# Second layer of a two-layer encoder: two projection chunks of 1024 columns in place of four of 512, rotation in place, attentions that take items as quarters come

## The chip, the cores and the metric

The kernel runs on one core of one Trainium2 chip. The metric is the device time of one execution in microseconds (us). A core has a matrix engine (TensorE, PE in the profile; its weight loads are PEld), VectorE (DVE), ScalarE (ACT), GpSimd (POOL) and a queue that only starts transfers (SP). Each works through its own instructions in order and waits for others by semaphores.

## The reference

Two layers over 512 tokens of width 1024, with 256 memory tokens. The second layer, which the change is about:

```python
h = rmsnorm(x, norm_g[i]); mem_h = rmsnorm(mem, mem_norm_g[i])
proj = einsum('bsd,de->bse', h, w_in_b)      # q 8 heads | k 2 | v 2 | q_mem 4 | gate 12, heads of 128
# mixer_axial_gqa, four q heads to one k/v head
q = rmsnorm(q, qn_g); k = rmsnorm(k, kn_g)
q = apply_rope(q, ang) * 128**-0.5; k = apply_rope(k, ang)
o_mix = softmax(q @ k.T) @ v
# memory_attention, 4 heads
q = rmsnorm(q_mem, qn) * 128**-0.5; k = rmsnorm(kv_k, kn)
o_mem = softmax(q @ k.T) @ kv_v
y = concatenate([o_mix, o_mem]) * silu(gate)
x = x + y @ w_out[i]
```

## The kernel before

All float32 products are made of three float32r matmuls (`mm3`: high x high, high x low, low x high), so every operand is split into a high part (a cast on ScalarE) and a low part (a subtraction on VectorE). For weights these are `wh` and `wo`, tiles of 128 x 1024.

The large projections run as *chunks* (`s_chunk`). A chunk takes the 512 tokens in two halves i and its columns in two halves j, so it has four quarters of output, named "11", "12", "21", "22" by i and j. It makes them with seven products (Winograd's form of Strassen's multiplication), in the order 12, 11, S1, S2, S4, S3, 22, on two accumulators in PSUM (`pj`). After a product `keep` copies the accumulator on ScalarE, or `add` combines it with a kept copy on VectorE (`sn<-pj,sn`); a quarter that is finished goes into its evaluation `ev`. Products S2, S4 and S3 go on accumulating in a bank that an eviction has read. Quarter 11 is finished after the second product, 12 after the fifth, 22 after the sixth, 21 after the seventh.

A product is cut into *slots*. A chunk of 512 columns (n = 256) has one slot per product: 24 matmuls that move 256 columns. A chunk of 1024 columns (n = 512) has two slots per product: 12 matmuls of 512 columns each. Each slot uses one pair `wh`, `wo`. Class `Weights` streams them: `dma` loads 512 KB tiles (`wl`) on SP's queue while fewer than `KEEP` of the chunk's kind live; the products T1 to T4 need sums of quarters, which `sum` makes with adding transfers on GpSimd's queue (T1 and T3 add from DRAM, `wl<-in_wall_dram`; T2 and T4 add from another tile, `wl<-wl`); `hi` and `lo` split them. `PLAN` lists the chunks' kinds.

Class `Driver` interleaves all else. After a slot's matmuls `tick` steps every spawned generator once, and up to two of the `later` ones; a `yield n` sleeps n slots. `drv.late` puts work at the end of the tick, `drv.soon` at the start of the next. So what stands in each engine's queue is set by this order alone. In the gate chunks a and b every third slot has a half tick more (`HALF`), which steps the first of the `later` generators.

The second layer has 79 slots: 8 for the memory's keys and values (`mem_kv`), four chunks of 512 columns for q_mem, k with v, and q in two halves, three gate chunks of 512 columns (m for the four memory heads, a for heads 0 to 3, b for heads 4 to 7), 14 slots of seven products of the output projection (`out_proj`) for the memory heads and heads 0 to 3, and 8 for the rest of it (`out_rest`, heads 4 to 7). Attentions are pipelines (`pipeline`) of five steps, one item per step:

- `score` on TensorE (`sb`; `sm` for memory); `top` takes the row maximum on VectorE (`nmb`, `nmm`);
- `exps` on ScalarE (`pb`, `pm`); `scale` on VectorE (`rdb` and `pb`; `rdm` and `pm`);
- `turn` transposes on TensorE (`ptb`, `pmt`), split by ScalarE and VectorE into `pbT`, `pmT`;
- `pv` on TensorE (`ob`, `om`), `out_` copies to `o` on ScalarE, and a transfer stores it in DRAM (`odb<-o`).

The attention of the mixer (`attn_b`) has 32 items, four blocks of 128 tokens in each of eight heads, in the order of the heads. The memory attention has eight. The evaluation of a gate quarter loads the stored outputs again (`og<-odb`) once they are there, and multiplies them in (`yf`). `prep_y` makes the seven operands of the output projection from `yf`: y12 and y11 need only the first half of the tokens, the others (`ys`, then `yS`) both halves. `rope_b` rotates q and k with the tables `ropeB` (tile `tabs`), which `setup_b` makes on GpSimd at the beginning of the layer.

Of the kernel before, what the change touches and what calls it, by code (L numbers as in the profile page):

```python
# [30 lines left out]
YB = {"m": (2, 2), "k": (1, 1, 1), 0: (1, 2, 1), 1: (1, 2, 1)}  # L31
# [4 lines left out]
PLAN = ["W2"] + ["T2"] * 2 + ["W1", "W2s"] + ["W2" if c.isdigit() else "W1" for c in A_ORDER[1:]] + ["W2"] + ["O1"] * 2 + ["T2b"] * 2 + ["W1b"] * 7 + ["W2b"] + ["O1"] * 2  # L36
T1_DMA = 17
KEEP = {"T2": 6, "T2b": 4, "O1": 4, "W1": 9, "W2": 10, "W2s": 9, "W1b": 7, "W2b": 9}
# [71 lines left out]
def trunk_kernel(ctx: ExitStack, tc: tile.TileContext, x, mem, wall, norm_g, mem_norm_g, gcol,  # L110
# [48 lines left out]
    LOADS = (("21", "21"), ("11", "11"), ("T1", "12"), ("T2", "22"), ("22", "22"), ("T3", "12"))  # L159
    GROUPS = {"T2": (2, 2), "T2b": (2, 2), "O1": (1, 4)}  # L160

    class Weights:
        def __init__(self):
# [3 lines left out]
            for c, kind in enumerate(PLAN):  # L167
                base = len(self.items)
                if kind in GROUPS:
                    units, nb = GROUPS[kind]  # L170
                    for u in range(units):
                        for x in (2 * u, 2 * u + 1):
                            self.items.append((c, "P", x))
                            self.last.append(g + (u + 1) * nb - 1)
                            self.allocs.append(((c, "P", x), d, kind))
                            self.users[c, "P", x] = 1
                            d += 1
                        self.need += [base + 2 * u + 2] * nb
                    g += units * nb
                else:  # L180
                    n = 1 if kind in ("W1", "W1b") else 2
                    at = {k: d + i * n for i, k in enumerate(("21", "11", "12", "22"))}
                    d += 4 * n
                    self.allocs += [((c, k, x), at[q] + x, kind) for k, q in LOADS for x in range(n)]
                    for k in ORDER:
                        for x in range(n):
# [3 lines left out]
                            if k[0] == "T":  # L190
                                self.sums.append(((c, k, x), at["11" if k == "T1" else "22"] + x))
# [17 lines left out]
        def dma(self, most=9):  # L209
            while self.allocs and self.live < KEEP[self.allocs[0][2]] and most:  # L210
# [7 lines left out]
                nc.sync.dma_start(self.tile[key], wall[d])  # L218
# [4 lines left out]
        def sum(self, force=False, want=None):  # L223

            for n, (key, d) in enumerate(self.sums[:8]):
# [3 lines left out]
                if k == "T1" and c >= T1_DMA:  # L229
                    if not self.ripe(self.load_at, key, force):  # L230
                        continue
                    G.dma_start(self.tile[key], wall[d], accum_op=ALU.add)
# [10 lines left out]
                elif k == "T3":  # L243
                    if not self.ripe(self.load_at, key, force):
                        continue
                    G.dma_start(self.tile[key], wall[d], accum_op=ALU.add)
# [84 lines left out]
    def s_chunk(n, act, ev, tokens=True, pre=None, half=False):  # L331
# [5 lines left out]
        def keep(name, u, b):  # L337
# [3 lines left out]
            if name == "s3":  # L341
                c = snap["s5", u]
                V.tensor_tensor(c, c, t, ALU.subtract)
                yield 1
                yield from ev("22", u, c)

        def add(q, name, u, b):
            t = snap[name, u]
            V.tensor_tensor(t, b, t, ALU.subtract if q == "12" else ALU.add)  # L349
            yield 1  # L350
# [3 lines left out]
        for i, (a, s, fresh) in enumerate(PRODUCTS):  # L354
# [4 lines left out]
            for x in range(units):  # L359
                wh, wo = [t.rearrange("p (k c) -> p k c", c=n) for t in W.take()]  # L360
                ah, al = act[a][:, 0], act[a][:, 1]
                for b in range(2):
# [6 lines left out]
                    o = bank[s][b] if units == 2 else bank[s][0][:, b * 256:(b + 1) * 256]  # L369
                    bs = slice(b * 128, (b + 1) * 128)  # L370
# [215 lines left out]
    def pipeline(n, *stages, ready=None, step=1):  # L586

        last = max(k for k, _, _ in stages)
        for t in range(n + last):
            while ready and t < n and not ready(t):  # L590
                yield 1
            for k, f, late in stages:
                if 0 <= t - k < n:
                    if late:
                        drv.late(lambda f=f, i=t - k: f(i))
                    else:
                        f(t - k)
            yield step

    def mem_attn(qm, km, vm, put, step):  # L600

        sc, pr, pts, tp, oo = {}, {}, {}, {}, {}

        def score(i):
            h, b2 = divmod(i, 2)
            sp = sc[i] = at("sm").rearrange("p (b k) -> p b k", b=2)
            for j in range(2):
                cs = slice((2 * b2 + j) * 128, (2 * b2 + j + 1) * 128)
                mm3(sp[:, j, :], qm[h // 2][0][:, h % 2, cs], qm[h // 2][1][:, h % 2, cs], km[0][:, h, :], km[1][:, h, :], True, True)
# [33 lines left out]
        def pv(i):  # L643
            h, b2 = divmod(i, 2)
            p = pts.pop(i)
            if b2 == 0:
# [6 lines left out]
        def out_(i):  # L653
            h, b2 = divmod(i, 2)
            if b2:
                os = put(h)
                A.copy(os, oo.pop(h))
                put(h, os)

        yield from pipeline(8, (0, score, 0), (4, pv, 0), (3, turn, 0), (2, scale, 0), (1, exps, 0),  # L660
                            (0, top, 1), (3, hi, 1), (3, lo, 1), (4, out_, 1), step=step)
# [20 lines left out]
    def gates(od, o_done):  # L682
# [3 lines left out]
        def gate(H, first, g, half=False):  # L686
# [6 lines left out]
            def ev(q, u, t):  # L693
# [7 lines left out]
                o = load() if {h0, h0 + 1} <= o_done else None  # L701
# [5 lines left out]
                if not o:  # L707
                    while not {h0, h0 + 1} <= o_done:
# [184 lines left out]
    def put_od(i, t=None):  # L893
# [3 lines left out]
        o_done.add(i)  # L897
# [20 lines left out]
    def mem_a():  # L918
        while seen[0] < 4:
            yield 1  # L920
        yield from mem_attn(qm, km, vm, lambda h, t=None: put_od(8 + h, t), MEM_STEP[0])
# [270 lines left out]
    def put_ob(i, t=None):  # L1192
# [279 lines left out]
```

## Time and profile before

| | |
|---|---|
| median of 3 timed runs | 997.8 us (997.62 to 1000.34) |
| the profiled execution: its time | 1000.03 us |
| the profiled execution: its span | 998.3 us |
| mean granted TensorE clock | 0.993 |
| TensorE, VectorE, ScalarE, GpSimd busy | 955.1, 821.6, 644.5, 340.2 us |
| first 256-wide matmul of the second layer | at 690.82 us |

A line of a timeline gives the start, the duration, the engine, the source line, the operation, the tiles written and read with their shapes, and in brackets the idle time before it with what ended it. A line of the groups gives the count after x, the busy time with the mean of one in ns, and the idle time before. A matmul's duration is a latency: the next one starts before it ends.

### The profile page before, as it was taken

To read this page: it belongs to the slowest core of one execution; us is meant where nothing else is said; L and a number is where in the kernel's file an instruction comes from. 1 tells how busy PE (TensorE), PEld (TensorE's weight loads), DVE (VectorE), ACT (ScalarE), POOL (GpSimd) and SP (SyncE) were. 2 spreads that over 40 slices of the span, in tenths; PEclk is the share of its full clock that TensorE was granted. 3 is DMA by queue.
4 is the path that set the end of the run, shared out by engine and by line. 5 is a ranking of instruction groups with operands and counts; after the bars stand their busy time and mean duration, and the time that the engine had idled before them with its cause. 6 is when DMAs were issued, how large, how long until landed. Compare 5 with 4: busy or idle time off the path is not lost.

```text
span 998.3 us, 16623 instructions
## 1 busy us (share of the span) xinstructions
PE 955.1 (96%) x5724; PEld 839.7 (84%) x5724; DVE 821.6 (82%) x1487; ACT 644.5 (65%) x1623; POOL 340.2 (34%) x470
## 2 busy tenths in 40 slices
PE   7899999999999999999999979999999999998998
PEld 4778988887888888888899967888999989987886
DVE  5787678778878787878888898978879898889974
ACT  4566568676768685858685646556667666667650
POOL 1232424665545454545544020223632331011000
PEclk9999999999999999999999999999999999999999
DMA  9969946959595949585949695759784876777432
GB/s 336 296 199 352 279 99 159 308 111 277 122 281 120 282 118 283 124 277 126 273 103 312 181 273 150 274 214 336 194 190 117 228 174 166 207 200 170 134 127 85
DMA packets 86966, 206.13 MB, mean 206 GB/s; under 512 B 25057, under 2 KB 35809, under 8 KB 86882
## 3 DMA queue, kind: packets, MB, share of 16 engines
q1 hardware_dynamic: 70034, 146.28, 41.3%
q0 software_dynamic: 15552, 56.63, 30.1%
q10 hardware_dynamic: 1296, 2.16, 0.6%
q8 instruction: 45, 0.74, 0.3%
q14 instruction: 39, 0.32, 0.1%
HBM read 157.79 MB, written 12.65 MB: 171 GB/s over the span
## 4 chain that ended last, share of the span: by engine, by line
PE 55%; DVE 14%; DMA 3%; ACT 3%; issue 3%; POOL 1%; SPq 0%; DVEq 0%; ACTq 0%; POOLq 0%
PE pj L149 13%; PE pj L148 13%; PE pj L150 13%; DVE wo L277 4%; PE oo L1102 1%; PE pt L1081 1%; DVE wl L236 1%; PE qT L512 1%; PE sa L1000 1%; DMA oth<-ds 1%; PE ptb L1304 1%; DVE sn L349 1%; DMA wl<-wl 1%; POOL tabs L1182 1%; PE xT L442 1%
## 5 line engine op out<-in xcount | busy, mean ns | idle before, releaser
L277 DVE TENSOR_TENSOR wo<-wl,wh 128x1024 fp32r<-128x1024 f32 x255 | 316.3, 1244 | 10.2 <-ACT wh L267 9.9
L267 ACT CAST wh<-wl 128x1024 fp32r<-128x1024 f32 x255 | 267.6, 1056 | 41.2 <-PE pj L150 20.8
L148 PE MATMUL pj<-wh,hS 128*128 128x512 f32 (+1 forms) x448 | 164.9, 368 | 4.3 <-DVE sn L349 3.3
L149 PE MATMUL pj<-wo,hS 128*128 128x512 f32 (+1 forms) x448 | 158.8, 354 | 2.7 <-DVE wo L277 2.6
L150 PE MATMUL pj<-wh,hS 128*128 128x512 f32 (+1 forms) x448 | 158.7, 354 | 0.0
L149 PE MATMUL pj<-wo,h 128*128 128x512 f32 (+1 forms) x336 | 120.1, 358 | 6.5 <-DVE wo L277 6.5
L148 PE MATMUL pj<-wh,h 128*128 128x512 f32 (+1 forms) x336 | 123.6, 368 | 1.7 <-ACT h L142 1.7
L150 PE MATMUL pj<-wh,h 128*128 128x512 f32 (+1 forms) x336 | 119.6, 356 | 0.0
L391 POOL TENSOR_TENSOR rstd<-mse,half 128x4 f32<-128x4 f32 (+2 forms) x98 | 106.3, 1085 | 8.2
L148 PEld LDWEIGHTS pj<-wh,hS 128*128 128x128 f32 x448 | 85.2, 190 | 14.9 <-DVE sn L349 3.8
L149 PEld LDWEIGHTS pj<-wo,hS 128*128 128x128 f32 x448 | 85.5, 191 | 13.9 <-DVE wo L277 4.1
L150 PEld LDWEIGHTS pj<-wh,hS 128*128 128x128 f32 x448 | 85.3, 190 | 12.1
L500 ACT ACTIVATE junk<-sn 128x128 f32<-128x128 f32 x264 | 78.9, 304 | 20.8 <-DVE sn L349 19.7
L390 POOL TENSOR_SCALAR mse<-hss 128x4 f32<-128x4 f32 (+1 forms) x86 | 47.9, 557 | 109.8 <-ACT junk L500 105.3
L149 PEld LDWEIGHTS pj<-wo,h 128*128 128x128 f32 x336 | 64.3, 191 | 16.5 <-DVE wo L277 9.1
L339 ACT COPY sn<-pj 128x512 f32<-128x512 f32 x132 | 72.5, 584 | 8.2 <-PE pj L150 8.2
L251 POOL DMA_DIRECT2D wl<-wl x33 | 29.8, 903 | 131.1 <-DVE wo L277 70.3
L944 POOL TENSOR_TENSOR ta<-sn,tabs 128x128 f32<-128x128 f32 (+1 forms) x64 | 36.5, 571 | 109.6 <-DVE sn L505 76.9
L148 PEld LDWEIGHTS pj<-wh,h 128*128 128x128 f32 x336 | 64.3, 192 | 9.5 <-ACT h L142 2.1
L150 PEld LDWEIGHTS pj<-wh,h 128*128 128x128 f32 x336 | 64.2, 191 | 9.0 <-DVE h L145 0.2
L349 DVE TENSOR_TENSOR sn<-pj,sn 128x512 f32<-128x512 f32 x99 | 67.6, 683 | 3.9 <-PE pj L150 3.9
L148 PE MATMUL pj<-hS,wh 128*128 128x256 f32 x192 | 56.8, 296 | 8.6 <-DVE sn L349 6.0
(226 smaller groups left out, 2449.0 us busy)
## 6 DMA issues: line engine op xcount, KB each, us to landing
wl<-in_wall_dram SPq DMA_DIRECT2D x222, 512.0 KB, 7.1
wl<-wl POOLq DMA_DIRECT2D x66, 512.0 KB, 5.5
wl<-in_wall_dram POOLq DMA_DIRECT2D x42, 512.0 KB, 8.6
od<-o SPq DMA_DIRECT2D x12, 256.0 KB, 4.3
og<-od SPq DMA_DIRECT2D x12, 256.0 KB, 6.9
odb<-o SPq DMA_DIRECT2D x12, 256.0 KB, 2.2
og<-odb SPq DMA_DIRECT2D x12, 256.0 KB, 3.6
x<-in_x_dram SPq DMA_DIRECT2D x4, 512.0 KB, 7.0
```

The source lines that it names most:

```text
L148: T.matmul(o, lh, rh, start=start, stop=False, skip_group_check=True)
L149: T.matmul(o, lh, rl, start=False, stop=False, skip_group_check=True)
L150: T.matmul(o, ll, rh, start=False, stop=stop, skip_group_check=True)
L251: G.dma_start(self.tile[key], self.tile[c, "T2", x], accum_op=ALU.add)
L267: A.copy(wh, self.tile[self.items[i]])
L277: V.tensor_tensor(wo, self.tile[key], wh.bitcast(F32), ALU.subtract)
L339: A.copy(t, b)
L349: V.tensor_tensor(t, b, t, ALU.subtract if q == "12" else ALU.add)
L390: G.tensor_scalar(e, ss, EPS, None, ALU.add)
L391: G.tensor_tensor(r, e, half[:, 0:n], ALU.pow)
L500: A.activation(jk, p[:, j * 128:(j + 1) * 128], AF.Square, scale=QS, accum_out=ss[:, j:j + 1])
L944: G.tensor_tensor(ta[:, 0:n], xn[:, 0:n, 0:32], ropeA[:, 0, b, s0:s0 + n], ALU.mult)
```

## The change

The four chunks of 512 columns become two of 1024. The first holds q_mem, k and v: its column half j = 0 is memory heads 0 and 1 with k, j = 1 memory heads 2 and 3 with v (`ev_mkv`). The second holds all q (`ev_q`), with heads 0, 1, 4, 5 in j = 0 and 2, 3, 6, 7 in j = 1. The host's layout of the weights stays, so a tile of a wide chunk is fetched from two blocks of DRAM, 512 columns of each (`PAIRS`, `like`). `rope_b` writes the product with the cosine over its input and needs one tile less. `spread` makes the evaluations of later blocks start one slot apart. `pipeline` no longer stops when its next item is not ready, and the items wait for quarters: memory items go by halves of the tokens (`BY_HALF`), those of the mixer in the order `ITEMS_B`: all eight heads of the first half of the tokens, then all of the second. Outputs are stored by halves, 24 transfers of 128 KB in place of 12 of 256 KB.

```diff
-PLAN = [...] + ["T2b"] * 2 + ["W1b"] * 7 + ["W2b"] + ["O1"] * 2
+PLAN = [...] + ["T2b"] * 2 + ["W2k", "W2q"] + ["W1b"] * 3 + ["W2b"] + ["O1"] * 2
-KEEP = {"T2": 6, "T2b": 4, "O1": 4, "W1": 9, "W2": 10, "W2s": 9, "W1b": 7, "W2b": 9}
+KEEP = {"T2": 6, "T2b": 4, "O1": 4, "W1": 9, "W2": 10, "W2s": 9, "W1b": 7, "W2b": 9, "W2k": 9, "W2q": 7}
...
+                    if kind in PAIRS:
+                        at = {(k, x): wall[d + i:d + i + 5:4, :, x * 512:(x + 1) * 512].rearrange("h p c -> p h c")
+                              for i, k in enumerate(QUARTERS) for x in range(2)}
...
-                yield 1
+                yield 1 + spread * u
                 yield from ev("22", u, c)
...
-            yield 1
+            yield 1 + (q == "21" and spread)
             yield from ev(q, u, t)
...
-        for t in range(n + last):
-            while ready and t < n and not ready(t):
-                yield 1
+        began, t, new = {}, 0, 0
+        while new < n or began:
+            if new < n and (not ready or ready(new)):
+                began[new] = t
+                new += 1
+            at_ = {t - b: i for i, b in began.items()}
...
+    BY_HALF = [(h, i) for i in range(2) for h in range(4)]
...
-                o = load() if {h0, h0 + 1} <= o_done else None
+                o = load() if {(h0, i), (h0 + 1, i)} <= o_done else None
...
+        sb = s2(name="sb").rearrange("p (a e) -> p a e", a=4)[:, 0:n]
+        V.tensor_tensor(sb, x, ropeB[:, qk, 1, b][:, None].to_broadcast([128, n, 128]), ALU.mult)
+        V.tensor_tensor(x, x, ropeB[:, qk, 0, b][:, None].to_broadcast([128, n, 128]), ALU.mult)
         yield d[1]
+        V.tensor_tensor(x[:, :, 0:64], x[:, :, 0:64], sb[:, :, 64:128], ALU.subtract)
+        V.tensor_tensor(x[:, :, 64:128], x[:, :, 64:128], sb[:, :, 0:64], ALU.add)
...
+    drv.later(mem_attn(lambda p, h, b: qm_b[b // 2][p][:, h, b % 2 * 128:b % 2 * 128 + 128], km, vm,
+                       lambda h, i=None, t=None: put_ob(8 + h, i, t), MEM_STEP[1], BY_HALF,
+                       lambda i: n_qm.get((i // 4, i % 4 // 2), 0) == 2))
+    s_chunk(512, H2, ev_mkv, half=HALF.get("kv"), spread=1, pair=True)
...
+    ITEMS_B = [(h, i) for i in range(2) for h in (0, 1, 4, 5, 2, 3, 6, 7)]
...
-                            ready=lambda i: n_rot[0] >= 8 + i // 16 * 4)
+                            ready=lambda i: sum(n_qm.values()) == 8 and n_q.get((i // 16, i // 8 % 2), 0) == 2)
...
+    drv.later(attn_b())
+    s_chunk(512, H2, ev_q, half=HALF.get("q"), spread=1, pair=True)
```

Three places show how instructions move. The first is GpSimd's queue at the beginning of the second layer. `tabs<-tbraw,grB` makes the rotation tables, `mse` and `rstd` belong to the norms of heads, the DMA rows are the adding transfers of `sum`. Before:

```order
L241 DMA wl<-wl 128x1024
L246 DMA wl<-in_wall_dram 128x1024
L251 DMA wl<-wl 128x1024
L232 DMA wl<-in_wall_dram 128x1024
L1182 TENSOR_TENSOR tabs<-tbraw,grB 128x512 x4
```

After:

```order
L243 DMA wl<-in_wall_dram 128x2x512
L403 TENSOR_SCALAR mse<-hss 128x4
L404 TENSOR_TENSOR rstd<-mse,half 128x4
L252 DMA wl<-wl 128x1024 x2
L262 DMA wl<-wl 128x1024 x2
L1210 TENSOR_TENSOR tabs<-tbraw,grB 128x512 x4
L257 DMA wl<-in_wall_dram 128x2x512 x2
```

Before, the first chunk's T3 (L246) stands ahead of the tables; after, both of its T3 additions (L257) stand behind them.

The second place is VectorE at the border of the q chunks and gate chunk m, from one `wo` to the next. `sn<-sn,rstd`, `sb<-sn,tabs` and `sn<-sn,tabs` are a norm and a rotation, L343 (before) and L354 (after) make quarter 22. Before, in a slot where `attn_b` runs:

```order
L277 TENSOR_TENSOR wo<-wl,wh 128x1024
L505 TENSOR_TENSOR sn<-sn,rstd 128x512
L1236 TENSOR_TENSOR ta<-sn,tabs 128x512
L1237 TENSOR_TENSOR sb<-sn,tabs 128x512
L1294 RECIPROCAL rdb<-denb 128x1
L1295 TENSOR_SCALAR pb<-pb,rdb 128x512
L1285 TENSOR_REDUCE nmb<-sb 128x1
L1313 TENSOR_TENSOR pbT<-ptb,pbT 128x4x128
```

After, in a slot there:

```order
L288 TENSOR_TENSOR wo<-wl,wh 128x1024
L518 TENSOR_TENSOR sn<-sn,rstd 128x512
L1229 TENSOR_TENSOR sb<-sn,tabs 128x512
L1230 TENSOR_TENSOR sn<-sn,tabs 128x512
L354 TENSOR_TENSOR sn<-sn 128x512 x2
L647 RECIPROCAL rdm<-denm 128x2
L649 TENSOR_SCALAR pm<-pm,rdm 128x256 x2
L1309 RECIPROCAL rdb<-denb 128x1
L1310 TENSOR_SCALAR pb<-pb,rdb 128x512
L636 TENSOR_REDUCE nmm<-sm 128x2
L664 TENSOR_TENSOR pmT<-pmt,pmT 128x512
L1300 TENSOR_REDUCE nmb<-sb 128x1
```

Memory items (`pm`, `nmm`, `pmT`) and items of `attn_b` (`pb`, `nmb`) now share slots.

The third place is VectorE ahead of S1 of the second layer's output projection, whose operand is `yS_11126` before and `yS_11181` after. Before:

```order
L277 TENSOR_TENSOR wo<-wl,wh 128x1024
L757 TENSOR_TENSOR ys<-yf 128x512 x2
L759 TENSOR_TENSOR ys<-ys,yf 128x512 x2
L1294 RECIPROCAL rdb<-denb 128x1
L1295 TENSOR_SCALAR pb<-pb,rdb 128x512
L1285 TENSOR_REDUCE nmb<-sb 128x1
L1313 TENSOR_TENSOR pbT<-ptb,pbT 128x4x128
L277 TENSOR_TENSOR wo<-wl,wh 128x1024
L741 TENSOR_TENSOR yS_11126<-ys,yS_11126 128x512 x2
```

After:

```order
L1328 TENSOR_TENSOR pbT<-ptb,pbT 128x4x128
L740 TENSOR_TENSOR yf<-sn,og 128x512
L784 TENSOR_TENSOR ys<-yf 128x512 x2
L786 TENSOR_TENSOR ys<-ys,yf 128x512 x2
L817 TENSOR_TENSOR acc<-sn,acc 128x512
L360 TENSOR_TENSOR sn<-pj,sn 128x512
L1309 RECIPROCAL rdb<-denb 128x1
L1310 TENSOR_SCALAR pb<-pb,rdb 128x512
L1328 TENSOR_TENSOR pbT<-ptb,pbT 128x4x128
L768 TENSOR_TENSOR yS_11181<-ys,yS_11181 128x512 x2
```

After, the last `yf` that S1 needs, with its loaded `og`, stands right ahead of `ys` and `yS`, and no `wo` lies between: on TensorE no projection matmul stands between `y11`'s last and S1's first.

More of the change, by code (lines that the diff above doesn't have):

```diff
@@ L643, in pv @@
         def pv(i):
[L644 removed]
+            h, b2 = order[i]
             p = pts.pop(i)
[L646 removed]
+            if h not in oo:
                 oo[h] = at("om")
```

199 lines of the change are left out of this document (94 added, 105 removed).

## The prediction

> **What bounds the kernel now.** I read the page first, then the second layer by stage, because the diff leaves the order of the first layer as it is.
>
> ```profile
> span 998.3 us, 16623 instructions
> PE 955.1 (96%) x5724; PEld 839.7 (84%) x5724; DVE 821.6 (82%) x1487; ACT 644.5 (65%) x1623; POOL 340.2 (34%) x470
> PE 55%; DVE 14%; DMA 3%; ACT 3%; issue 3%; POOL 1%; SPq 0%; DVEq 0%; ACTq 0%; POOLq 0%
> ```
>
> TensorE is the bound and VectorE the next one: it holds 14% of the chain that ended last. The table by stage splits the second layer into the four chunks of 512 columns, the three gate chunks, the first seven products of the output projection, and the rest.
>
> ```profile
> 690.80:799.10 108.30, 104.03 (x860) 103.35 (x858) 91.77 (x141) 74.15 (x203) 42.34 (x44) 0.98 0.75 192
> 799.10:908.30 109.20, 104.09 (x805) 99.42 (x804) 95.87 (x166) 70.06 (x148) 18.32 (x19) 1.00 0.72 182
> 908.30:965.50 57.20, 53.38 (x280) 44.95 (x279) 52.50 (x87) 35.47 (x65) 2.63 (x3) 0.97 0.50 148
> 965.50:998.30 32.80, 27.71 (x121) 22.26 (x119) 16.65 (x25) 5.38 (x7) 0.00 (x0) 1.00 0.25 94
> ```
>
> The columns after the length are busy TensorE, weight loads, VectorE, ScalarE, GpSimd; then granted clock, DMA share, GB/s. VectorE is within 5 us of TensorE in the third stage and 8 us behind in the second, so a few microseconds more of VectorE at one place make it the bound there. TensorE's waits are few, and the timeline of PE names them:
>
> ```profile
> 702.59 0.39 PE L148 MATMUL pj<-wh,hS 128*128 128x256 f32 x1 [1.17 <-DVE sn L349]
> 727.71 0.39 PE L148 MATMUL pj<-wh,hS 128*128 128x256 f32 x1 [0.95 <-ACT sn L339]
> 782.84 0.39 PE L148 MATMUL pj<-wh,hS 128*128 128x256 f32 x1 [2.15 <-DVE sn L349]
> 812.51 0.39 PE L148 MATMUL pj<-hS,wh 128*128 128x256 f32 x1 [2.06 <-DVE sn L349]
> 923.25 0.50 PE L148 MATMUL pj<-wh,y 128*128 128x512 f32 x1 [3.37 <-DVE sn L349]
> 974.03 0.50 PE L150 MATMUL pj<-wh,y 128*128 128x512 f32 x1 [1.10 <-DVE y L721]
> ```
>
> Nearly all are waits for an eviction (`sn`) that stands behind other work in VectorE's queue.
>
> **Term 1, the width of the matmuls.** The four chunks issue 224 groups of three 256-wide matmuls (L148, L149, L150 have equal counts), so 672; after the change 336 do the same work at 512 wide.
>
> ```profile
> L148 PE MATMUL pj<-wh,hS 128*128 128x256 f32 x128 | 37.4, 292 | 4.3 <-DVE sn L349 3.3 <-ACT sn L339 1.0
> ...
> L148 PE MATMUL pj<-wh,h 128*128 128x256 f32 x96 | 27.9, 291 | 0.0
> ```
>
> The mean of 291 ns is a latency. The step between starts counts, from 24 steps of the narrow and nine of the wide form:
>
> ```profile
> 704.00 0.28 PE L150 MATMUL pj<-wh,hS 128*128 128x256 f32 x1
> ...
> 706.88 0.28 PE L150 MATMUL pj<-wh,hS 128*128 128x256 f32 x1
> ...
> 119.75 0.39 PE L150 MATMUL pj<-wh,h 128*128 128x512 f32 x1
> ...
> 121.79 0.39 PE L150 MATMUL pj<-wh,h 128*128 128x512 f32 x1
> ```
>
> 2.88 / 24 = 0.120 us and 2.04 / 9 = 0.2267 us. So 672 x 0.120 = 80.6 us become 336 x 0.2267 = 76.2 us: **-4.5 us**, all of it on the path as long as TensorE bounds. The Trainium skill (TensorE: Matmul & The Clock Gate, "Wait — 56ns, not 53.3ns?") gives N / 2.4 GHz plus about 2.5 ns per step; an estimate from it is 109 and 216 ns, and a saving of 0.9 us, not 4.5. The rows show a larger fixed part, 13 ns, and they decide.
>
> **Term 2, waits inside the four chunks.** With two banks per accumulator a product fills two slots, so an eviction has one slot more before its bank is written again. The waits at 702.59 and 727.71 go: -2.1 us. One comes: the two T3 additions of the first wide chunk now stand on GpSimd's queue behind the rope tables.
>
> ```profile
> 702.02 7.98 POOL tabs L1182 x4
> ...
> wl<-in_wall_dram POOLq DMA_DIRECT2D x42, 512.0 KB, 8.6
> ```
>
> The tables end at 710.0; two issues of 1 to 1.5 us and 8.6 us to land put them at about 720 and 721. ScalarE's casts of them stand ahead of the `keep` copies of S2, and product S3 (slot 10 of the chunk, due at about 690.8 + 29.8 = 720.7) needs those copies. I take +1.5 us, between 0 (landing 2 us sooner) and 3. Net **-0.6 us**. The other edits here are small: rotation in place writes the same elements; keys, values and memory queries come in halves of 256 columns, which adds some 2.5 us of VectorE and 1.6 us of ScalarE in a stretch where both have time, and two `rstd` pairs on GpSimd. The weights' bytes are the same in runs of 2 KB in place of 4. Cost zero, covered by TensorE; uncovered they are in rival C.
>
> **Term 3, VectorE where both attentions meet.** Before, the eight memory items end before the first of the 32 items of `attn_b`. After, memory items wait for quarters of q, and the last four run with the first items of `attn_b` and with the rotations of the late q quarters. The steps of VectorE:
>
> ```profile
> 848.00 0.69 DVE L349 TENSOR_TENSOR sn<-pj,sn 128x512 f32<-128x512 f32 x1
> 848.61 0.15 DVE L1294 RECIPROCAL rdb<-denb 128x1 f32<-128x1 f32 x1
> 848.79 0.49 DVE L1295 TENSOR_SCALAR pb<-pb,rdb 128x512 f32<-128x512 f32 x1
> 849.20 0.69 DVE L1285 TENSOR_REDUCE nmb<-sb 128x1 f32<-128x512 f32 x1
> 849.80 0.68 DVE L1313 TENSOR_TENSOR pbT<-ptb,pbT 128x512 fp32r<-128x512 f32 x1
> 850.39 1.22 DVE L277 TENSOR_TENSOR wo<-wl,wh 128x1024 fp32r<-128x1024 f32 x1
> 851.53 0.69 DVE L713 TENSOR_TENSOR yf<-sn,og 128x512 f32<-128x512 f32 x1
> ...
> 779.58 0.34 DVE sn L1240
> ...
> 894.01 0.45 PE ptb L1304 x4
> ```
>
> From start to start: 0.60 for 512 columns, 0.19, 0.41, 1.14 for `wo`, 0.34 for 256 columns; a transpose on TensorE is 0.11. In the order after, eight slots (from the second-last of the q chunk on) hold 8 `wo`, 49 operations of 512 columns, 7 `pb`, 18 of 256 and 11 reciprocals: 9.1 + 29.4 + 2.9 + 5.6 + 2.1 = 49 us. TensorE's in the same slots: 48 x 0.227 + 204 x 0.12 + 56 x 0.11 = 41.5 us. So VectorE is 7.6 us over. The same count for before, over nine slots, gives 41.8 us against 39.3 of TensorE, and the stretch lasted 41.65:
>
> ```profile
> 799.07:840.72 41.65, 39.59 (x311) 37.88 (x308) 39.15 (x67) 26.82 (x62) 11.39 (x11) 1.00 0.71 170
> ```
>
> VectorE was idle for 2.5 us of it, so the count is a little high; I take 6 us, between 0 (the queue runs behind without anyone waiting) and 7.6. A wait of this size also costs clock. In these slices the granted clock falls right after a wait:
>
> ```profile
> 780.00:785.00 5.00, 2.85 (x23) 2.61 (x22) 4.93 (x10) 3.77 (x12) 2.41 (x3) 0.94 0.74 180
> 785.00:790.00 5.00, 5.00 (x34) 5.00 (x34) 2.38 (x5) 1.46 (x3) 3.48 (x4) 0.72 0.80 244
> 920.00:925.00 5.00, 1.75 (x6) 1.45 (x7) 4.96 (x11) 3.07 (x7) 0.47 (x1) 0.94 1.01 183
> 925.00:930.00 5.00, 5.00 (x25) 4.44 (x24) 4.42 (x8) 1.52 (x5) 0.00 (x0) 0.72 0.13 25
> ```
>
> 5 x 0.06 + 5 x 0.28 = 1.7 us lost each time, after 2.15 and 3.37 us of waiting. The Trainium skill (the same page, "HAM oscillation — how this bites in real kernels") warns of idle gaps above about 3.4 us; here 2.15 us were enough. By the rule the new waits of this term would cost no clock, and the sum would be 1.7 us less. What goes: 2.15 + 2.06 + 1.7 = 5.9. What comes: 6 + 1.7. Net **+1.8 us**.
>
> **Term 4, the output projection waits for the last half.** Before, heads run one after another, and heads 0 to 3, which the seven products need, are done long before. After, all first halves of the tokens run ahead of all second halves. Product S1 needs the second half of heads 2 and 3, items 24 to 27. In the order after, TensorE comes to S1 with four steps of the pipeline between, in which it has only `ob` and `ptb`. Followed by hand from the end of the `ob` of items 26 and 27 (time 0): `o` copied at 1.4, after the `pbT` copy ahead of it; store and load by these rows:
>
> ```profile
> odb<-o SPq DMA_DIRECT2D x12, 256.0 KB, 2.2
> ...
> og<-odb SPq DMA_DIRECT2D x12, 256.0 KB, 3.6
> ...
> 965.52 3.56 DMA og<-odb
> ```
>
> 1.4 + 2.2 + 3.6 = 7.2. Then on VectorE, in the order shown: `yf`, four `ys`, `acc`, `sn`, `pbT`, two `yS` at 0.6, `rdb` and `pb` together 0.6: 6.6, so S1's operand is there at 13.8. TensorE has 1.44 us of `ob` and four times 0.44 of `ptb` in that time: 3.2. It waits 10.6, and 1.0 more at S2, behind four `yf` and a `wo`: 11.6. The waits at 923.25, at 974.03 and one of 0.45 go (4.9); the clock loss is there in both. **+6.7 us** (bounds: 3, if the clock of the chain starts earlier, and 9).
>
> **Sum.** -4.5 - 0.6 + 1.8 + 6.7 = +3.4 us. The profiled execution took 1000.03 us (span 998.3), so it would take 1003.4; it stood 2.2 us above the median of 997.8. Against the median: 1001.2, say **1001.5 us**. 0.3% (3 us) is about what a measurement can tell from no change.
>
> **Rivals.** A, faster: VectorE's backlog in term 3 delays nobody, since `wo` is made over two slots ahead, and the T3 additions land in time. Then -4.5 - 2.1 - 5.9 + 6.7 = -5.8: 992.0 us. It decides at a backlog of one slot's projection matmuls (24 x 0.12 = 2.9 us): each step's transposes need the step before. For it: the wide chunks give evictions a slot more. Against it: the 2.06 us wait at 812.51, where the excess was only 2.5. Chance 0.27.
> B, nothing: term 4 comes out at its lower bound 3. Then -0.3: 997.5. Chance 0.05.
> C, late weights: the q chunk keeps seven tiles alive as a narrow chunk did, but four of them (two of quarter 21, two of T2) stay for most of it, so its second T2 is added only two slots ahead of its cast, where a narrow chunk has three. Two late casts of some 2 us each, with ScalarE's queue behind them, and one loss of clock: +5, 1006.5. Speaks for it: the `wl<-wl` landing on the chain in the first chunk. Chance 0.15.
> D: a wide step costs twice a narrow one (0.240), so term 1 is nothing: 1005.7. The rows at 119.75 and 121.79 speak against it. Chance 0.03. By the step of the Trainium skill's clock-gate page, quoted in term 1, the sum would be 3.6 us later than the forecast's, 1004.8.
>
> **Chances.** The forecast has 0.50, of which 0.38 lies above +3 us and 0.12 within. Rival A gives 0.24 faster and 0.03 same, B 0.05 same, C and D 0.18 slower. Faster 0.24, same 0.20, slower 0.56. The range for 8 in 10 goes from rival A to the forecast with terms 3 and 4 at their upper ends and some of C: 991.5 to 1010.
>
> **What would show it.** Right: a stretch of 8 to 12 us with few matmuls ahead of the first `yS` product in the second layer, released by VectorE behind a DMA `og<-odb`; VectorE at 100% and TensorE with waits at the border of the q chunk and the first gate chunk; steps of 0.227 us in the two wide chunks. Wrong: no waits at that border (A), or ScalarE's `wh` waiting for DMA in the q chunk (C).

## The result and the profile after

The changed kernel takes 1008.31 us (median of 6 runs, 1006.0 to 1011.63); the kernel before, run beside it, 997.71 us. The ratio is 1.0098, 95% interval [1.0084, 1.0113]: about 10 us slower, where 3.7 us slower was forecast. The time lies in the forecast's range and on its side, but nearly three times as far from the kernel before. The profiled execution took 1011.33 us, 11.3 more than that of before; it is one of the longer of the six.

From the page:

```profile
span 1009.5 us, 16024 instructions
PE 957.9 (95%) x5388; PEld 823.7 (82%) x5388; DVE 824.4 (82%) x1505; ACT 644.9 (64%) x1635; POOL 339.6 (34%) x474
```

TensorE has 336 matmuls less and VectorE is as busy as before. The stages with the same borders as in the prediction's table: the wide chunks, the gate chunks, the output projection up to product S3, the rest (length; busy PE, PEld, DVE, ACT, POOL; clock, DMA share, GB/s):

```profile
691.90:794.58 102.68, 97.94 (x488) 81.28 (x487) 84.08 (x136) 69.61 (x192) 42.78 (x44) 0.98 0.79 197
794.58:918.70 124.12, 116.34 (x885) 109.96 (x883) 112.21 (x203) 80.05 (x183) 18.11 (x22) 0.99 0.65 167
918.70:978.47 59.77, 50.52 (x236) 41.70 (x234) 49.15 (x76) 31.96 (x56) 1.75 (x2) 0.89 0.48 148
978.47:1009.50 31.03, 27.36 (x121) 22.34 (x119) 14.27 (x20) 4.13 (x5) 0.00 (x0) 0.98 0.17 68
```

To tell work from waiting I count each stage's matmuls by their steps (0.2267, 0.120, and 0.11 us for a transpose). What is left of the stage's length is its loss: waits, and steps at a lower clock.

| | start | chunks | gates | projection to S3 | rest | sum |
|---|---|---|---|---|---|---|
| length, change | +1.1 | -5.6 | +14.9 | +2.6 | -1.8 | +11.2 |
| work, change | | -7.5 | +9.2 | -6.0 | 0 | -4.4 |
| loss before | | 6.4 | 5.6 | 6.7 | | |
| loss after | | 8.3 | 11.3 | 15.3 | | |

Work has moved from the chunks and from the projection into the gate chunks, because memory items run later and the 32 items end earlier. In sum it is 4.4 us less, as forecast. The losses ate it nearly four times over. TensorE's longest waits, from its timeline:

```profile
677.37 0.50 PE L149 MATMUL pj<-wo,act 128*128 128x512 f32 x1 [1.80 <-DVE wo L288]
724.19 0.50 PE L148 MATMUL pj<-wh,hS 128*128 128x512 f32 x1 [1.95 <-ACT sn L350]
798.84 0.39 PE L149 MATMUL om<-pmT,vm 128*128 128x256 f32 x1 [1.11 <-DVE pmT L664]
802.05 0.66 PE L1319 MATMUL ptb<-ident,pb 128*128 128x128 f32 x4 [1.21 <-ACT pb L1304]
895.79 0.58 PE L148 MATMUL pj<-hS,wh 128*128 128x256 f32 x1 [2.46 <-DVE sn L360]
938.65 0.38 PE L148 MATMUL ob<-pbT,vb 128*128 128x256 f32 x1 [3.13 <-ACT pbT L1323]
952.63 1.11 PE L1319 MATMUL ptb<-ident,pb 128*128 128x128 f32 x4 [3.45 <-DVE pb L1310]
```

In order: a wait ahead of the chunks that was not there before; the T3 wait in the first wide chunk; two of seven short ones (5.7 us in all) where memory items and `attn_b` meet; an eviction behind the y operands; and two of the five largest ahead of the first yS product, which starts at 953.40. Behind some of them the granted clock drops:

```profile
725.00:730.00 5.00, 5.00 (x16) 3.95 (x15) 3.96 (x7) 2.68 (x4) 0.00 (x0) 0.66 0.52 174
895.00:900.00 5.00, 4.21 (x23) 4.21 (x24) 4.78 (x10) 2.59 (x5) 0.87 (x1) 0.66 0.52 163
940.00:945.00 5.00, 3.86 (x18) 2.89 (x16) 4.77 (x10) 2.78 (x8) 0.00 (x0) 0.66 0.59 132
950.00:955.00 5.00, 2.37 (x8) 2.08 (x9) 4.96 (x11) 2.33 (x5) 0.00 (x0) 0.50 0.12 43
```

### The profile page after: what moved, and what is told of

It reads as the page before. It is cut to its first block, busy times and chain, and to the rows that moved or that the text cites. A ratio compares the mean times of both kernels' runs of the same rounds, so it can differ in the third digit from the quotient of the medians.

```text
span 1009.5 us, 16024 instructions
## 1 busy us (share of the span) xinstructions
PE 957.9 (95%) x5388; PEld 823.7 (82%) x5388; DVE 824.4 (82%) x1505; ACT 644.9 (64%) x1635; POOL 339.6 (34%) x474
## 5 line engine op out<-in xcount | busy, mean ns | idle before, releaser
L288 DVE TENSOR_TENSOR wo<-wl,wh 128x1024 fp32r<-128x1024 f32 x255 | 315.4, 1239 | 15.6 <-ACT wh L278 15.3
L148 PE MATMUL pj<-wh,hS 128*128 128x512 f32 (+1 forms) x384 | 153.9, 401 | 2.5 <-ACT sn L350 1.9
L149 PE MATMUL pj<-wo,hS 128*128 128x512 f32 (+1 forms) x384 | 147.7, 385 | 2.3 <-DVE wo L288 2.2
L150 PE MATMUL pj<-wh,hS 128*128 128x512 f32 (+1 forms) x384 | 147.4, 384 | 0.0
L149 PE MATMUL pj<-wo,h 128*128 128x512 f32 (+1 forms) x288 | 111.8, 388 | 6.5 <-DVE wo L288 6.5
L148 PE MATMUL pj<-wh,h 128*128 128x512 f32 (+1 forms) x288 | 115.3, 400 | 1.5 <-ACT sn L350 0.8
L150 PE MATMUL pj<-wh,h 128*128 128x512 f32 (+1 forms) x288 | 111.1, 386 | 0.0
L403 POOL TENSOR_SCALAR mse<-hss 128x4 f32<-128x4 f32 (+1 forms) x88 | 45.8, 520 | 134.3 <-ACT junk L513 130.0
L149 PEld LDWEIGHTS pj<-wo,hS 128*128 128x128 f32 x384 | 72.8, 190 | 15.8 <-DVE wo L288 3.7
L148 PEld LDWEIGHTS pj<-wh,hS 128*128 128x128 f32 x384 | 72.7, 189 | 15.7 <-ACT sn L350 2.4
L150 PEld LDWEIGHTS pj<-wh,hS 128*128 128x128 f32 x384 | 72.7, 189 | 14.9
L149 PEld LDWEIGHTS pj<-wo,h 128*128 128x128 f32 x288 | 55.0, 191 | 18.1 <-DVE wo L288 9.1
L148 PEld LDWEIGHTS pj<-wh,h 128*128 128x128 f32 x288 | 54.9, 191 | 11.2 <-ACT sn L350 1.2
L150 PEld LDWEIGHTS pj<-wh,h 128*128 128x128 f32 x288 | 54.8, 190 | 11.0 <-DVE h L145 0.2
```

The source lines that it names most:

```text
L148: T.matmul(o, lh, rh, start=start, stop=False, skip_group_check=True)
L149: T.matmul(o, lh, rl, start=False, stop=False, skip_group_check=True)
L150: T.matmul(o, ll, rh, start=False, stop=stop, skip_group_check=True)
L288: V.tensor_tensor(wo, self.tile[key], wh.bitcast(F32), ALU.subtract)
L403: G.tensor_scalar(e, ss, EPS, None, ALU.add)
```

## The experiments

Every ratio is to the kernel before on the same chip, with its 95% interval; the changed kernel's own is 1.0098. A thousandth is one microsecond. The intervals reach 1 to 2 us to each side, so where two of them overlap a difference of 2 or 3 us between two changed kernels is not shown by the ratios. Of an edit that touches one stage the trace of that stage tells more, since the start of the second layer differs by up to 3 us between profiled runs of kernels that have the same first layer. But each trace is one execution, and a drop of the clock behind a wait comes in some executions and not in others (the last section shows when); it makes a stage some 1.5 us longer, so I compare stages with their clocks.

**The order of the second halves.**

```diff
-    ITEMS_B = [(h, i) for i in range(2) for h in (0, 1, 4, 5, 2, 3, 6, 7)]
+    ITEMS_B = [(h, 0) for h in (0, 1, 4, 5, 2, 3, 6, 7)] + [(h, 1) for h in range(8)]
...
-                            ready=lambda i: sum(n_qm.values()) == 8 and n_q.get((i // 16, i // 8 % 2), 0) == 2)
+                            ready=lambda i: sum(n_qm.values()) == 8 and n_q.get((ITEMS_B[i // 2][1], ITEMS_B[i // 2][0] % 4 // 2), 0) == 2)
```

> Edit: the changed kernel with the second halves of the heads taken in the order 0 to 7 (in place of 0, 1, 4, 5, 2, 3, 6, 7), so that product S1 of the output projection needs items up to 23 instead of 27, some three slots (13 us) sooner. Theory (term 4: S1 waits for the last items of heads 2 and 3): the waits ahead of the first yS product and the clock that they cost go; the stage from the first y12 product to the last yS3 product falls from 59.8 us to about 51, and the time by 8 to 11 us, to 997.5 to 1000.5. Rival (the stage is long because all items come late and crowd VectorE and ScalarE, whatever their order): the waits stay in another place, 0 to 3 us come back, 1005.5 to 1008.5.

Measured: 1.0067 [1.0048, 1.0086], 3 us less, where the theory gave 8 to 11. The stage, and on TensorE and ScalarE what stayed:

```profile
917.34:972.42 55.08, 47.74 (x235) 39.21 (x234) 46.63 (x73) 32.43 (x58) 1.75 (x2) 0.97 0.55 160
938.64 0.39 PE L148 MATMUL ob<-pbT,vb 128*128 128x256 f32 x1 [3.13 <-ACT pbT L1323]
935.33 0.62 ACT L746 CAST y<-sn 128x512 fp32r<-128x512 f32 x1 [5.64 <-PE sb L149]
```

The stage is 4.7 us shorter, not 9: the theory holds half. The operand of S1 is written at 933.4, yet its product starts at 942.28. In between stands a wait that I had not seen: ScalarE's cast of `y`, the last gate's operand, waits 5.64 us for a matmul of the *scores*. The changed kernel has the same (5.32 us, until the same 935.33). `y` has nothing to do with scores. By the tiles' addresses, as I worked them out, one of the four y tiles lies where the low part of the keys lay (L149 reads it), and L149 of the last item is its last reader; the next run tests that. ScalarE's queue stands there, with the `pbT` copy and the weight casts behind it.

**Another place for y.** One weight tile fewer ahead for the last chunk shifts which buffers come free when; the y tiles then take over old weights and probabilities.

```diff
-KEEP = {... "W2b": 9, ...}
+KEEP = {... "W2b": 8, ...}
```

> Edit: the changed kernel with 8 instead of 9 weight tiles of the last product's chunk held ahead, nothing else. The four y tiles of the last gate chunk then come to lie in buffers that are free before; in the changed kernel two of them take over a low part of q and the low part of the keys (kbT), which TensorE reads until the last score. Theory (ScalarE's queue stands 5.3 us at a cast of y until the last score has been read, and the pbT copies, casts of weights and copies of accumulators behind it come late): that wait goes, the 3.3 us wait of ob at 935 with it, and 3 to 5 us of the stage, 1003.5 to 1005.5. Rival (the chain through the items of heads 2 and 3 is as long without it, as the prediction had it): TensorE waits as long at another place, within 1 us of 1008.5.

Measured: 1.0119 [1.0105, 1.0134]: no gain (2 us more, but the intervals overlap). SP's queue first of the changed kernel, then of this one; then VectorE and TensorE of this one:

```profile
943.32 0.32 SPq L1223 DMA_DIRECT2D odb<-o  x1
945.03 0.37 SPq L725 DMA_DIRECT2D og<-odb  x1
```

```profile
934.10 1.27 SPq L809 DMA_DIRECT2D acc<-x1d  x2
936.71 0.32 SPq L1223 DMA_DIRECT2D odb<-o  x1
941.91 0.37 SPq L725 DMA_DIRECT2D og<-odb  x1
947.67 0.69 DVE L740 TENSOR_TENSOR yf<-sn,og 128x512 f32<-128x512 f32 x1 [7.99 <-DMA og<-odb]
952.62 1.11 PE L1319 MATMUL ptb<-ident,pb 128*128 128x128 f32 x4 [9.32 <-DVE pb L1310]
```

ScalarE no longer waits at y (its longest wait for a cast of y is 0.71 us), and the output of heads 2 and 3 is stored 6.6 us sooner (936.71 for 943.32). But `yf` comes at 947.67 in both. The store of 128 KB takes 5.2 us until the load of 256 KB behind it can go, not 1.7, and the load lands 5.7 us later, not 2.6. Two loads of 512 KB (`acc<-x1d`) and a weight tile went out just ahead; in the changed kernel they had gone 12 us ahead of the store. That these transfers slow it is read from the order and not tested. The rival's time is right; its reason, a chain of fixed length, is not.

**Both.**

> Edit: both the sorted second halves of the earlier run (heads 0 to 7) and 8 weight tiles held ahead. Theory (order and buffer each cost part of the last stage): the losses from the first y12 product to the last yS3 product fall from 15.3 us to about 6 (before the change: 6.7), and the time to about 999, 1000 at most. Rival (the order alone is what counts and the buffer nothing): 1005.5 as with the order alone. Rival 2 (the buffer alone counts): as in the run with 8 tiles alone.

Measured: 1.0037 [1.0023, 1.0051], 6 us less than the changed kernel. The stage is 8.0 us shorter, nearly what the theory had (9); of its time, 8 to 9 us less, 2 to 3 us are missing.

```profile
917.76:969.54 51.78, 46.29 (x235) 37.73 (x234) 46.55 (x73) 32.06 (x56) 1.75 (x2) 1.00 0.61 180
```

The loss of the stage is 7.6 us (changed kernel 15.3, before 6.7), and the granted clock is whole. Alone the two edits give -3 us and no gain, together -6: S1 waited for two chains side by side, and taking one away shows the other.

**The rope tables, sooner.**

```diff
-SET_B = ... 11
+SET_B = ... 5
```

> Edit: the changed kernel with the rope tables on GpSimd issued 6 slots earlier (delay 5 instead of 11), so that the two T3 additions of the first wide chunk do not stand behind them. Theory (term 2): the wait of 2.1 us at 721.9 goes, and the clock loss of 1.7 us in the slices behind it: 3.8 us less, 1004.5. Rival 1 (the clock falls at the next wait anyway): 2 us less, 1006.3. Rival 2 (the additions are late by the transfers themselves, not by GpSimd's queue): no change, 1008.3.

Measured: 1.0162 [1.014, 1.0185], 6 us more. None of the three expectations had that.

```profile
695.20 1.09 PE L525 MATMUL qT<-ident,xn 128*128 128x128 f32 x4 [4.56 <-DVE xn L518]
701.40:800.06 98.66, 96.04 (x489) 80.21 (x488) 81.72 (x134) 69.86 (x192) 34.04 (x40) 1.00 0.78 187
```

The chunks became 4.0 us shorter with the clock at 1.00, so the theory's price for this stage was right. But the tables now stood ahead of an `rstd` of the memory's keys on GpSimd, and TensorE waited 4.56 us for it, with the clock at 0.51 from 695 to 700 behind it: the chunks begin at 701.40 instead of 691.90.

**The rope tables, later.** The same line, 13 instead of 11.

> Edit: the changed kernel with the rope tables on GpSimd two slots later (delay 13 instead of 11), so that the two T3 additions stand ahead of them in its queue. Nothing ahead of the chunks moves, as it did when the tables came six slots earlier. Theory (term 2): the wait of 2 us at 722 and the clock loss of 1.7 us behind it go, the first keys wait for the tables while TensorE has other work: 3 to 4 us less, 1004.5 to 1005.5. Rival (the late tables make the first keys, and the rotation behind them, late by the same amount): no change, 1008.5.

Measured: 1.008 [1.0067, 1.0092], 2 us less; the intervals overlap.

```profile
693.38:792.04 98.66, 96.03 (x488) 80.22 (x487) 84.05 (x136) 69.86 (x192) 42.32 (x44) 1.00 0.83 205
```

The same 4.0 us in the stage (98.66 for 102.68). Not all of that is the wait. In the kernel with the sorted second halves the T3 wait is still there (1.75 us), but no drop of the clock came behind it, and its chunks took:

```profile
692.35:793.21 100.86, 96.31 (x488) 80.14 (x487) 83.99 (x136) 69.64 (x192) 43.54 (x44) 1.00 0.81 200
```

So the wait is worth 2.2 us in the stage without a drop and about 4 with one, and over many executions the gain lies between. Of seven profiled kernels with this wait four had the drop.

**Fewer tiles ahead in the first wide chunk**, for the 1.80 us wait at 677.37. VectorE stands there until a store of x1, the layer's input, has read `acc`, which it then normalises in place.

```diff
-"W2k": 9
+"W2k": 7
```

> Edit: the changed kernel with 7 instead of 9 weight tiles held ahead for the first wide chunk. SP's queue then has four loads instead of six between the two last pairs of stores of x1 (the kernel before has four). Theory (the wait of 2 us at 675, for wo behind a VectorE that waits for the last store, comes from the two loads that SP issues ahead of it): that wait goes, 1.5 to 2 us less, about 1006.8. Rival (fewer tiles ahead make the first wide chunk's additions and casts late): waits of 2 us or more inside the chunk, 1008.5 or more.

Measured: 1.0126 [1.0107, 1.0145], 3 us more.

```profile
726.25 0.80 PE L148 MATMUL pj<-wh,hS 128*128 128x512 f32 x1 [4.48 <-ACT sn L350]
690.18:796.44 106.26, 98.31 (x489) 81.03 (x487) 87.99 (x136) 69.40 (x192) 43.19 (x46) 0.98 0.81 195
```

Theory and rival both came true: the wait at 677 is gone and the chunks begin at 690.18, but the T3 wait grew from 1.95 to 4.48 us. The ratios' intervals overlap; the stage, 3.6 us longer at the same clock, shows the loss.

**The low parts of the first eight items.** This kernel leaves out a part of the product, so it is for its time alone.

```diff
...
         def lo(i):
             b2, j = divmod(i, 2)
+            if i < 8:
+                return
...
-                    mm3(o, vb[0][:, k, es], vb[1][:, k, es], pT[0][:, k], pT[1][:, k], k == 0, k == 3)
+                    mm3(o, vb[0][:, k, es], vb[1][:, k, es], pT[0][:, k], pT[-1][:, k], k == 0, k == 3)
```

> Edit: the changed kernel without the low part of the transposed probabilities for the first 8 of the 32 items of the second attention (the matmuls take the high part twice; TensorE's work is the same). It leaves out 8 VectorE operations of 512 columns, 8 x 0.6 = 4.8 us, in the slots where memory items and attention items meet. Theory (term 3: VectorE is over TensorE there, and the waits of 6.5 us in all between 797 and 818 are its backlog): 3 to 5 us less, 1003.3 to 1005.3. Rival (the backlog delays nobody, the waits are the latency of the chain from step to step): within 1 us of 1008.3.

Measured: 1.009 [1.0072, 1.0108], 0.8 us less. The ratio alone speaks for the rival. The stage does not:

```profile
795.44:916.00 120.56, 114.48 (x884) 108.46 (x883) 106.89 (x195) 79.96 (x183) 18.33 (x22) 1.00 0.66 172
```

It is 3.6 us shorter than in the changed kernel, but with the clock at 1.00, where the changed kernel had a drop behind the wait at 895.79. The run with 8 tiles has the same order in this stage and no drop either:

```profile
794.46:917.09 122.63, 114.91 (x884) 108.52 (x883) 112.05 (x203) 80.10 (x183) 18.30 (x22) 1.00 0.65 165
```

Against that the stage is 2.1 us shorter, for 4.8 us of VectorE taken away. VectorE's backlog does cost there, less than the theory's 3 to 5; the two longest of the early waits (1.11 and 1.21 us in the changed kernel) stayed as they were. How much of the 2.1 us reaches the end is open within the ratio's interval.

**The width alone.** Every wide matmul as two narrow ones, once in the changed kernel:

```diff
-                        if tokens:
+                        if pair:
+                            for x_ in range(2):
+                                mm3(o[:, x_], ah[:, kk, bs], al[:, kk, bs], wh[:, k, x_], wo[:, k, x_], st and not x_, sp)
+                        elif tokens:
```

> Edit: the changed kernel with every 512-wide matmul of the two wide chunks issued as two of 256, everything else as it is: 672 matmuls in place of 336. Theory (term 1: steps of 0.120 and 0.2267 us): 4.5 us more, 1012.8. Rival D (a wide step costs two narrow ones): no change, 1008.3. By the fixed part of 2.5 ns per step that the Trainium skill gives (TensorE: Matmul & The Clock Gate, "Wait - 56ns, not 53.3ns?"), an estimate would be 0.9 us more.

Measured: 1.0128 [1.0106, 1.015], 3.0 us more, known to 2.6 us either way. And once in the fastest kernel below:

> Edit: the fastest of the changed kernels so far (sorted second halves, 8 tiles held ahead, tables behind the T3 additions, x1 stored from ScalarE, y operands two slots later) with every 512-wide matmul of the two wide chunks issued as two of 256. In it the wide chunks have 1.5 us of waits less to hide anything under. Theory (term 1 in full: 672 steps of 0.120 in place of 336 of 0.2267): 4.5 us more than that kernel, a ratio to the kernel before of 1.0024. Rival (part of the narrow steps' time is hidden under waits that stay, as the 3 us of the first such run suggest): 2 to 3 us more, 1.000 to 1.001.

Measured: 1.0008 [0.9998, 1.0018], where that kernel has 0.9979: 2.9 us more, known to 1.4. The chunks of the two:

```profile
691.62:795.43 103.81, 99.73 (x825) 98.53 (x822) 84.97 (x136) 69.68 (x192) 43.88 (x44) 1.00 0.79 194
```

```profile
691.11:792.97 101.86, 99.53 (x825) 98.53 (x823) 84.25 (x136) 69.82 (x192) 42.39 (x44) 1.00 0.81 200
```

By its steps the work grows by 4.5 and 4.4 us, the stage by 1.1 and by 3.2. In the first pair some 1.7 us that are missing are the clock: the changed kernel had a drop in its chunks (0.98), the narrow one none (1.00). The rest is waits that shrink when TensorE is slower, about 1 us in either pair. Rival D (nothing) is out.

**What can be had together.** Sorted second halves, 8 tiles ahead, tables after the T3 additions:

> Edit: the changed kernel with the sorted second halves, 8 weight tiles held ahead for the last chunk and the rope tables behind the T3 additions, all three. Theory (the gains stand in different stages and add up: 6 us from the first two, 2 to 4 from the tables): 999 to 1001 where the kernel before has 998 to 999, a ratio of 1.000 to 1.002. Rival (the tables' gain is hidden by the later stages, since items then start earlier but run at the pace of VectorE): 1.0037 as without the tables.

Measured: 1.0007 [0.9995, 1.0019]. The gains add up, and the tables' gain is now clear of the noise: 3.0 us less than without them (1.0037). Then the stores of x1 from ScalarE's queue:

```diff
-                nc.sync.dma_start(x1d[b][:, j * 512:(j + 1) * 512], x1[j])
+                nc.scalar.dma_start(x1d[b][:, j * 512:(j + 1) * 512], x1[j])
```

> Edit: as the run with three edits together, and the stores of x1 issued from ScalarE's queue instead of SP's, behind the loads of weights no more. Theory (the 2 us wait at 675 comes from two more loads ahead of the last stores on SP's queue): it goes without touching the first wide chunk, 1.5 to 2 us less than the run with three edits. Rival (the store itself is slow among the loads, from whatever queue it is issued, or ScalarE loses as much by issuing): the wait stays, no difference.

Measured: 0.9999 [0.9987, 1.001], no clear difference, and the wait is still there, so the theory of SP's queue falls:

```profile
666.98 0.39 ACTq L1177 DMA_DIRECT2D x1d<-acc  x1
674.60 0.75 DVE L449 SCALAR_TENSOR_TENSOR acc<-acc,rstd,row 128x512 f32<-128x512 f32 x1 [0.58 <-DMA x1d<-acc]
676.54 0.50 PE L149 MATMUL pj<-wo,act 128*128 128x512 f32 x1 [2.09 <-DVE wo L288]
```

The store lands 7.6 us after its issue. Fewer loads in flight took the wait away, another queue did not. The Trainium skill (DMA: Bandwidth & Descriptors, "Queues, rings and completion order") has each transfer engine take packets from the queues in turn. By that a store on a queue of its own still shares the engines with the loads; 7.6 us, against up to 8.9 from SP's queue, agree with a sharing that gains little, but no run here tests it. Last, the y operands two slots later (`PREP_B` 3 instead of 1):

> Edit: as the run with x1 stored from ScalarE, and the preparation of the y operands started two slots later (delay 3 instead of 1). Theory (the wait of 2.4 us at 892 for an eviction is VectorE's backlog behind the low parts of y12 and y11, which stand at one place with two weight casts and an attention item; the clock falls behind it): moved two slots, it goes: 2.5 to 4 us less than that run. Rival (VectorE is over TensorE in the whole last gate chunk, and the y operands then press on y12, y11 or S1): the wait comes back at the first y12 or yS1 product, no change or slower.

Measured: 0.9979 [0.9969, 0.999], 996.88 us where the kernel before has 999.12: 2 us faster than the kernel before, and by the ratios 12 us faster than the changed one.

```profile
890.83 0.39 PE L148 MATMUL pj<-hS,wh 128*128 128x256 f32 x1 [1.06 <-DVE sn L360]
692.37:791.00 98.63, 96.00 (x488) 80.23 (x486) 84.00 (x136) 69.77 (x192) 42.28 (x44) 1.00 0.83 206
791.00:912.28 121.28, 114.92 (x884) 108.53 (x883) 111.90 (x203) 79.93 (x183) 18.36 (x22) 1.00 0.65 167
912.28:964.06 51.78, 46.24 (x236) 37.73 (x234) 46.33 (x73) 32.03 (x56) 1.74 (x2) 1.00 0.60 180
```

The wait at the y operands, 2.27 us in the run with x1 stored from ScalarE, is 1.06, and the gate stage 1.3 us shorter (121.28 for 122.63); neither of the two profiles has a drop of the clock there. The three stages shown have the clock at 1.00.

## Why the prediction was right in its side and short in size

| part | forecast | profiled |
|---|---|---|
| start of the chunks | 0 | +1.1 |
| work of the matmuls (term 1) | -4.5 | -4.4 |
| losses in the chunks (term 2; of term 3 the wait at 782.84 and its clock) | -0.6 - 2.15 - 1.7 = -4.45 | +1.9 |
| losses in the gate chunks (the rest of term 3) | 6 + 1.7 - 2.06 = +5.6 | +5.7 |
| output projection (term 4) | +6.7 | +8.6 - 1.8 = +6.8 |
| sum | +3.4 | +11.1 |

The steps that failed are term 2, with the credit that term 3 took from the same stage, and the start.

**Term 2** was mis-sized by 6.4 us. The waits at 702.59, 727.71 and 782.84 went as forecast. The T3 wait came where it was put, product S3 for ScalarE's copies behind the casts, but cost 4.0 us and not 1.5 (both runs that moved the tables): 1.95 us of waiting and a clock drop behind it. I charged a drop to the waits of term 3 and none to this one, against my own row in which 2.15 us had been enough. A drop for every wait of 2 us would have been too simple as well: my own row of 2.06 us at 812.51 stands in a stage with the clock at 1.00, and the T3 wait itself brought a drop in four of seven profiled kernels. By the rule of the Trainium skill (TensorE: Matmul & The Clock Gate, "HAM oscillation — how this bites in real kernels"), with gaps above about 3.4 us, 1.95 us would have cost none; this trace does not agree. Most of the rest are short waits inside the chunks (at 701, 762 and 769, 2.8 us in all; the last, 1.5 us, for a memory item's `pmT`, which term 3 looked for only at the border).

**The start** was called free: "cost zero, covered by TensorE". Two more loads in flight, by the new `KEEP`, keep a store from landing, 1.8 to 2.2 us in every kernel with nine tiles ahead. I had counted bytes and not what else is on its way at that moment. The +1.1 us of the table is less sure than the wait: starts of kernels with the same first layer differ by more.

**Term 3** came to its number, partly by chance. VectorE works without a pause from 793 to 816 and TensorE waits at the border, as forecast; without the eight low parts the stage is 2.1 us shorter at the same clock, so at least that much of the loss there is VectorE's. The early waits came to 5.7 us, near the 6 of the forecast, but no drop of the clock followed them, for which I had charged 1.7. Instead 2.46 us and a drop came at 895.79, at the y operands. I had followed that collision only as the 3.37 us at 923.25 that would go; that it is the same one, moved, is my reading and not tested. And two waits of the kernel before that my list does not have are gone as well:

```profile
848.75 0.39 PE L148 MATMUL pj<-hS,wh 128*128 128x256 f32 x1 [1.23 <-DVE sn L349]
898.85 0.39 PE L148 MATMUL pj<-hS,wh 128*128 128x256 f32 x1 [1.82 <-ACT sn L339]
```

In VectorE's count the 18 operations of 256 columns come to 6.1 us at 0.34 each, not 5.6; the 6 us that I took do not hang on it.

**Term 4** held in place and came to its size: the waits ahead of yS1, the last released by VectorE behind `og<-odb`:

```profile
947.68 0.69 DVE L740 TENSOR_TENSOR yf<-sn,og 128x512 f32<-128x512 f32 x1 [1.55 <-DMA og<-odb]
```

The five waits ahead of yS1 (what starts are further apart than a step) sum to 10.6 us, against 11.6 forecast for S1 and S2. The makeup was not the forecast's, and that the sum fits is luck: 3.9 us of them are ahead of the `ob` from which I counted, at ScalarE's cast of y, and after it TensorE waits 6.7 and not 10.6. No S2 wait of 1.0 came. The loss of clock, which I had put at the same before and after, grew: 0.89 in the stage for 0.97. The forecast's single chain was two, and the sorted order alone could not show it.

**Rivals.** A falls: the backlog does delay, and the additions came late (ScalarE's cast waited 4.05 us for the second, until 722.61). C falls: no `wh` in the q chunk waits for a transfer. D falls by the two narrow runs. By the step of the Trainium skill (TensorE: Matmul & The Clock Gate, "Wait — 56ns, not 53.3ns?") they should, by an estimate, have cost 0.9 us; they cost 3.0 and 2.9, with 4.4 to 4.5 by their steps. The interval of the first run leaves room for 0.9, that of the second does not.

## What to carry to other kernels

When a reordered pipeline makes a consumer wait, look for a second chain beside the one that the trace names: here a reused buffer held ScalarE for 5 us and a late transfer held VectorE, and taking away either alone gave nothing or half. Follow every operand's buffer to the last reader of what lay there before, since a longer life of one tile becomes a wait of an unrelated one. And an edit that is said to cost nothing because bytes or instructions are the same has moved what is in flight: price it at the queue where it now stands, and charge each wait of about 2 us that it makes with the clock that it can cost (here 1.7 us, or nothing).

## What was not expected of the hardware

A wait's length alone did not tell whether the clock falls. In the changed kernel 1.95 us at 724.19 was followed by 0.66 in the next five microseconds; with both edits together TensorE waits 1.83 us at one place of the projection, and the stage has 1.00 throughout:

```profile
943.11 0.63 PE L1319 MATMUL ptb<-ident,pb 128*128 128x128 f32 x4 [1.83 <-DVE pb L1310]
```

What decides is how the wait falls into fixed windows. In each of the 14 traces all changes of the granted clock lie whole multiples of 3.41 us apart, and a drop is to 0.50 for 3.41 us or a multiple of that. Here is one and the same wait of 2.27 us at the y operands in the run with three edits and in the one with x1 stored from ScalarE. Behind each row of the wait stand two of these windows, with TensorE's busy time after the length:

```profile
892.51 0.58 PE L148 MATMUL pj<-hS,wh 128*128 128x256 f32 x1 [2.27 <-DVE sn L360]
889.13:892.54 3.41, 1.14 (x8) 0.72 (x7) 3.39 (x6) 3.41 (x8) 0.00 (x0) 1.00 1.06 288
892.54:895.96 3.42, 3.42 (x16) 3.42 (x17) 3.40 (x6) 1.83 (x4) 0.93 (x2) 0.50 0.81 230
```

```profile
891.06 0.39 PE L148 MATMUL pj<-hS,wh 128*128 128x256 f32 x1 [2.27 <-DVE sn L360]
886.65:890.07 3.42, 2.14 (x16) 1.71 (x14) 3.42 (x6) 3.42 (x8) 0.00 (x0) 1.00 1.01 275
890.07:893.48 3.41, 2.42 (x20) 2.42 (x21) 3.37 (x7) 2.85 (x6) 0.86 (x1) 1.00 0.86 248
```

In the first all 2.27 us lie in one window, and the next runs at half clock; in the second a window's end cuts them into 1.28 and 0.99, and nothing follows. Over all 14 traces, from 35 us on and by the profile's busy time, of the windows at full clock each of the 32 in which TensorE stood idle for 1.93 us or more was followed by a drop, 6 of the 26 between 1.66 and 1.87, and none of the 67 between 1.2 and 1.65. So a wait of 2 us costs 1.7 us of clock or nothing, by where it falls; one of 1.2 us, alone in its window, cost none.

A store of 128 KB to DRAM and the load of 256 KB behind it took 4.3 us in the changed kernel (1.7 and 2.6) and 10.9 us behind two loads of 512 KB (5.2 and 5.7). So the medians from which the prediction took the price of such a hop (2.2 and 3.6) do not give that of one hop; that the loads just ahead made the difference is read from the order and not tested.
